# HGRN2's second head requests its state and rows behind columns that GpSimd writes; units 0 and 1 update their samples later

## Chip, cores and metric

The kernel runs on one core of a Trainium2 chip. The metric is the device time of one execution in microseconds. A run of the kernel before and one of the changed kernel are compared by the median over rounds on the same chip.

## What is computed

One inference step of a decoder layer for two groups that share the weights: a prompt of 16 meta and 256 prompt tokens, and 8 samples of one new token each, which bring recurrent states from earlier. Together they are 280 columns (in the code LP = 272 of the prompt, NS = 8 of the samples). The layer is a half feed-forward, the mixer, and a second half feed-forward, each with a layer norm. The mixer is what matters here:

```python
q_r, k_r, v_r, g_r, q_h, f_h, i_h, g_h, a_r, a_h = jnp.split(x @ w_in, N_PROJ, axis=-1)
f = lb + (1.0 - lb) * jax.nn.sigmoid(f_h.astype(jnp.float32))
k_h = to_heads((1.0 - f).astype(x.dtype), H_HG)
s_ret, o_r = retention_chunk(s_ret, q_r, k_r, v_r)
s_hg, o_h = hgrn2_chunk(s_hg, q_h, k_h, i_h, logf)
y = jax.nn.sigmoid(a_r) * o_r + jax.nn.sigmoid(a_h) * o_h
return y @ w_out, s_ret, s_hg
```

For each sample and each of the 16 HGRN2 heads the state of 128x128 becomes S' = f S + k v (an outer product of the new key and value), is written out, and gives the sample's output q S'. The 8 retention heads do the same with states of 256x256 and a fixed decay. The prompt goes through the chunked form of both and also leaves its last states.

## The kernel before

**Stages.** The span divides into the first feed-forward (up to about 745 us), the mixer's input projections with all of its recurrent work (745 to 1794), the output projection (to 1882), and the second feed-forward. Weights come from HBM in pieces of 128x1024 float32 (`raw`, 512 KB, three buffers). ACT rounds each to the matmul's format (`whi`, line 188), DVE makes the remainder (`wlo`, line 189), and PE runs 24 matmuls on it (line 218), three for each of 128 rows by 128 columns: whi with the high and the low part of x, wlo with the high part. All ten projections are made this way; their accumulators are called `pj_q_r`, `pj_i_h` and so on (r: retention, h: HGRN2).

**Units and threads.** The projections are made in eight units, u = 0 to 7. A unit covers 256 columns of each projection, one retention head and two HGRN2 heads (h = 0, 1). The recurrent work of a unit runs in two generators: `mix_hg(u, ...)`, started when a unit's `i_h` is ready, and `mix_ret(u, ...)`, started when its `v_r` is. A hook of the projections' loop, `pump`, goes on with the running generators after each step of six matmuls; `yield n` in a generator means that its next part comes n steps later. So the yields fix where the generators' matmuls stand between those of the projections.

**Order on the engines.** PE's order is the program's. On DVE, ACT and GpSimd (POOL) a scheduler orders instructions by what they depend on and by priority, and SP, which requests nearly all DMAs, has one queue in order: a request that has to wait holds all those behind it, the weights among them.

**The HGRN2 generator** (`mix_hg`). K and Q are scaled level by level with products of forget gates. A burst of small matmuls (`pl`, lines 823 and 849) makes the scores, which DVE copies into `acch` under masks (`fill`, lines 828 and 834) and ACT copies for the larger blocks (`keep`). `load(h)` requests the states of the 8 samples of head h (`smh`, 512 KB, line 769); `values(h)` requests the samples' value rows, repeated over the 128 partitions (`vbh`, 512 KB, line 772). The tiles of `smh` and `vbh` have two buffers each, which they share with the scaled queries `Qm` and with copies of K (`kept`). `turned(h)` transposes the scaled keys of head h (`ptk`, copied by ACT to `kth`, line 968). `gate()` transposes the samples' gates and keys (`ptm`) and prepares the first block's keys (`km`, line 255). `samples(h)` updates the 8 sample states of a head, each with a scaling on ACT (line 983) and a multiply-add on DVE (line 984), and requests the write of the new states (`out_sgs`, line 987). Then come the prompt's states (`pst`, `Sh`, lines 1013 to 1018), the product of the queries with the samples' new states (`pq`), and the prompt's output (`po`).

**Two paths.** Units 2 to 7 are called steady: they turn the keys of both heads first, then call the gate, then update head 0, and four steps later head 1. Units 0 and 1 call the gate first, and then turn and update head by head, two steps apart.

**The retention generator** (`mix_ret`), on the same engines: updates of its sample states (`smr`, lines 1180 to 1186, with repeated rows `vbr`), the samples' scores (`pqr`, then `scr`, line 240, and `sc`, lines 255, 723 and 724), their outputs (`osr`, centred at lines 1069 to 1071), and the output accumulator `por`: per head four matmuls of the prompt (line 1214), one of the samples' own values with `sc`, and one that adds `osr` (line 741).

Of the kernel before, what the change touches and what calls it, by code (L numbers as in the profile page):

```python
# [128 lines left out]
def trunk(ctx: ExitStack, tc: tile.TileContext, A, O):  # L129
    nc = tc.nc  # L130
# [12 lines left out]
    def mx_bank(name):  # L143
        return ps_m.tile([P, 512], F32, tag="mx", name=name)
# [135 lines left out]
    class Norm:  # L280
# [96 lines left out]
        def first(self, block, outs, x0s):  # L377


            n = self.n  # L380

            def hook(k):
                if k == 5:
                    self.stats()

            dense(block, KC, outs, xh, xl, [slice(x0, n + 2) for x0 in x0s], hook)
            ys = self.corrected(outs, x0s)
            for c in range(KC):
                d = self.d[c]
                sub(d, d, self.mean)  # L390
                nc.vector.scalar_tensor_tensor(
                    out=d, in0=d, scalar=self.g[:, c : c + 1], in1=self.r, op0=ALU.mult, op1=ALU.mult)
            return ys

        def second(self, block, outs, x0s, into=()):
            dense(block, KC, outs, xh, xl, [slice(x0, self.n + 2) for x0 in x0s])
            self.normalise()
            return self.corrected(outs, x0s, into)
# [148 lines left out]
    with tc.tile_pool(name="yp", bufs=1) as yp:  # L547
# [7 lines left out]
        with tc.tile_pool(name="mp", bufs=1) as mp:  # L555
# [7 lines left out]
            def tmp(name, shape=(P, T), bufs=1, dt=F32, tag=None):  # L563
                if name in rows:
                    rows[name] = rows[name][1:] + rows[name][:1]
                    return rp.tile(list(shape), dt, tag=rows[name][-1], name=name)
                return mp.tile(list(shape), dt, tag=tag or name, name=name, bufs=bufs)
# [80 lines left out]
            def evacuate(n, c0, c1, o0, o1, b0, b1):  # L648
# [14 lines left out]
                elif n == "i_h":  # L663
                    v = st.pop("i_h", None)
                    if v is None:
                        v = tmp("v", (P, 2, T))
                        nc.scalar.copy(v[:, 0, :], o0)
                        nc.scalar.copy(v[:, 1, :], o1)

                    start(mix_hg(c0 // 2, st["f"], st["k"], st["q"], v), {0: 20, 2: 46}.get(c0, 4))  # L670
                elif n in ("q_r", "k_r"):
                    sc, w, x0 = (1.0, TL, NMETA) if n == "q_r" else (KSC, T, 0)
# [48 lines left out]
            def upper_upper_lower(out, x, at=0):  # L721
                n = x.shape[0]
                nc.scalar.copy(out[:n], x)
                nc.scalar.copy(out[32 : 32 + n], x)
                sub(out[64 : 64 + n], x, out[at : at + n].bitcast(F32))
# [20 lines left out]
            def mix_hg(u, f, k, q, v):  # L746

                calm = 2
# [13 lines left out]
                acc = tmp("acch", (P, 2 * SEQ))  # L762
                sms, vbs = [], []

                def load(h):

                    sms.append(tmp("smh", (P, NS, P), bufs=2))
                    vbs.append(tmp("vbh", (P, NS, P), bufs=2))
                    nc.sync.dma_start(sms[h], A["sg"][2 * u + h])

                def values(h):
                    nc.sync.dma_start(vbs[h], vrow[h].partition_broadcast(P))


# [21 lines left out]
                def join(s):  # L796
                    _, m, t2 = sides(s)
                    Ts[2 * s] = tmp(f"T{2 * s}", (P, 2, m))
                    mul(Ts[2 * s], t2[:, :, :, 0], t2[:, :, :, 1])
# [25 lines left out]
                def fill(half, s, h):  # L825
                    a = acc[:, 2 * P * h : 2 * P * (h + 1)]
                    if s == 1:
                        nc.vector.tensor_tensor(
                            out=a.rearrange("p (b j c) -> p b j c", b=2, j=4),
                            in0=half[:, :, 48:].unsqueeze(2).to_broadcast([P, 2, 4, 32]),  # L830
                            in1=ident.rearrange("p (j c) -> p j c", j=4).unsqueeze(1).to_broadcast([P, 2, 4, 32]), op=ALU.mult)
                    for i, (sl, mi) in enumerate(((s, MASKS[s][0]), (2 * s, MASKS[2 * s][0]), (2 * s, MASKS[2 * s][1]))):
                        n = 16 // sl
                        nc.vector.copy_predicated(
                            a.rearrange("p (b j n t s) -> p b j n t s", b=2, j=4, t=2, s=sl)[:, :, :, :, 1, :],
                            msk[:, mi, :P].rearrange("p (b j n s) -> p b j n s", b=2, j=4, s=sl),
                            half[:, :, 16 * i : 16 * i + 16].rearrange("p b (n s) -> p b n s", s=sl).unsqueeze(2).to_broadcast([P, 2, 4, n, sl]))
# [15 lines left out]
                def keep(pl, s):  # L853
                    if s == 64:
                        for b in range(2):
                            nc.scalar.copy(
                                acc[:s, :].rearrange("p (h b n s) -> p h b n s", h=2, b=2, s=s)[:, :, b, 1, :],
                                pl[b * s : (b + 1) * s, : 2 * s].rearrange("p (h s) -> p h s", h=2))
                    else:
                        for j in range(0, 128 // s, 2):  # L860
                            nc.scalar.copy(
                                acc[j * s : (j + 1) * s, :].rearrange("p (x n s) -> p x n s", x=4, s=s)[:, :, j + 1, :],
                                pl[j * s : (j + 1) * s, : 4 * s].rearrange("p (x s) -> p x s", x=4))
# [20 lines left out]
                steady = u > 1  # L884
# [57 lines left out]
                scale_k(64)  # L942
                scale_q(64)
                join(64)
                for todo in (load, values):
                    for h in range(2):
                        todo(h)
                for h in range(2):
                    if u:
                        fill(first(h), 1, h)  # L950
                    fill(second(h), 4, h)
                    yield 4
                for s in (16, 32, 64):
                    keep(tops[s], s)
                yield 2 if steady else 8 if u else 4
                Tt = Ts[2 * LEVELS[-1]]
                on = tmp("on_h", (P, 2, TL), bufs=2)
                on_h[u] = on
                kts = []

                def turned(h):
                    kt = tmp("kth", (P, 2, P), bufs=2)
                    kts.append(kt)
                    pt = mx_bank("ptk")
                    for b in range(2):
                        t0 = NMETA + b * P
                        nc.tensor.transpose(pt[:, b * P : (b + 1) * P], K[:, h, t0 : t0 + P], ident)
                    nc.scalar.copy(kt, pt[:, : 2 * P].rearrange("p (b f) -> p b f", b=2))

                def gate():  # L970
                    pt = mx_bank("ptm")
                    x = pt[:64, :P]
                    nc.tensor.transpose(x, meta.rearrange("p h t -> p (h t)"), ident)
                    for i in range(2):
                        nc.gpsimd.tensor_copy(meta[:, :, NMETA + NS * i : NMETA + NS * (i + 1)], fk[:, i])
                    for i in range(2):
                        upper_upper_lower(km[:, i, :], x[32 * i : 32 * i + NMETA], 32 * i)

                def samples(h):
                    vb, sm = vbs[h], sms[h]  # L980
                    for b in range(NS):
                        at = NMETA + b
                        nc.scalar.activation(sm[:, b, :], sm[:, b, :], AF.Copy, scale=meta[:, h, at : at + 1])
                        nc.vector.scalar_tensor_tensor(
                            out=sm[:, b, :], in0=vb[:, b, :], scalar=meta[:, h, at + NS : at + NS + 1], in1=sm[:, b, :],
                            op0=ALU.mult, op1=ALU.add)
                    nc.sync.dma_start(O["sgs"][2 * u + h], sm)

                if steady:
                    turned(0)  # L990
                    yield 2
                    turned(1)
                    yield 4
                    gate()
                    samples(0)
                    yield 4
                    samples(1)
                    yield 6
                else:
                    gate()  # L1000
                    yield 7 if u else 6
                    for h in range(2):
                        turned(h)
                        samples(h)
                        yield 2
                    yield 12 + calm if u else 8

                Ss = []
                for h in range(2):
# [9 lines left out]
                            out=S[:, b + 1, :], in0=S[:, b, :], scalar=Tt[:, h, b : b + 1],  # L1019
                            in1=pst[:, (b + 1) * P : (b + 2) * P], op0=ALU.mult, op1=ALU.add)  # L1020
                    nc.sync.dma_start(O["sgp"][2 * u + h], S[:, 2, :])
                yield 53 if steady else 10
                pq = mx_bank("pq")
                for h in range(2):
                    for b in range(NS):
# [30 lines left out]
                calm = calm if u else 0  # L1056
# [308 lines left out]
```

## Time and profile before

| | us |
|---|---|
| runs | 2593.94, 2594.21, 2598.13 |
| median | 2594.21 |
| the profiled execution | 2599.28 |
| its span | 2597.5 |
| PE busy in it | 2564.2 |
| DVE busy | 1703.4 |
| ACT busy | 1392.9 |
| POOL busy | 42.0 |

The span is the time between the first and the last instruction of the profiled execution; the execution's own time has a start and an end around it. The profiled execution is one of its own, some 5 us longer than the median of the runs. PE's busy time is modelled: a matmul of 280 columns is listed with 0.28 us but the next one starts 0.12 us later. A row of a timeline gives the start, the duration, the engine, the line, the operation with its output and inputs, the shapes, the count, and in brackets how long the engine was idle before and whose end released it. In a table of windows stand busy times by engine, the granted clock of PE, the DMA engines' share and their rate.

### The profile page before, as it was taken

The numbers are of one execution on the slowest core, as the hardware profiler recorded it, in microseconds if no ns is written. First come the engines' busy times: TensorE is split into PE (matmuls) and PEld (weight loads), VectorE is DVE, ScalarE is ACT, GpSimd is POOL, SyncE is SP. The second block draws the span as 40 slices with busy tenths as digits, with TensorE's granted clock in tenths as the row PEclk, the third lists the DMA queues.
The fourth block names the chain that finished last, engine by engine and source line by source line (L and its number), as shares of the span: only waits on it lengthen the run. The fifth ranks groups of instructions, "written<-read, shape, count | busy, mean of one in ns | idle before, by whom it ended". The sixth has DMA issues, their size and how long they took to land.

```text
span 2597.5 us, 56210 instructions
## 1 busy us (share of the span) xinstructions
PE 2564.2 (99%) x23424; PEld 2544.3 (98%) x23424; DVE 1703.4 (66%) x2827; ACT 1392.9 (54%) x2186; POOL 42.0 (2%) x120
## 2 busy tenths in 40 slices
PE   9999999999999999999999999999999999999999
PEld 9999999999999889999999999999999999999998
DVE  6544454565579788777777777777985555556555
ACT  5444444444456667666666666665564444444444
POOL 0000000000000000000000000000000000000000
PEclk9999999999999999999999999999999999999999
DMA  7555555555566776767686868576556666666664
GB/s 241 186 184 183 186 185 183 184 184 183 185 198 209 237 263 217 263 200 265 196 269 196 269 196 268 195 250 188 194 187 199 196 195 196 195 195 194 196 195 148
DMA packets 156896, 536.26 MB, mean 206 GB/s; under 512 B 17952, under 2 KB 25952, under 8 KB 156640
## 3 DMA queue, kind: packets, MB, share of 16 engines
q1 hardware_dynamic: 156352, 532.37, 63.5%
q8 instruction: 183, 3.00, 0.5%
q14 instruction: 73, 0.60, 0.1%
q10 hardware_dynamic: 288, 0.29, 0.0%
HBM read 501.99 MB, written 30.61 MB: 205 GB/s over the span
## 4 chain that ended last, share of the span: by engine, by line
PE 90%; DVE 5%; ACT 2%; issue 1%; DMA 1%; SPq 0%; POOL 0%; DVEq 0%; ACTq 0%
PE up L218 34%; PE dn L218 18%; PE pj_k_r L218 3%; PE pj_g_r L218 3%; PE pj_q_r L218 3%; PE wo L218 3%; PE pj_a_r L218 3%; PE pj_v_r L218 3%; PE pj_g_h L218 3%; PE pj_a_h L218 3%; PE pj_q_h L218 3%; PE pj_i_h L218 3%; PE pj_f L218 3%; DVE wlo L189 2%; DMA raw<-in_w_up 1%
## 5 line engine op out<-in xcount | busy, mean ns | idle before, releaser
L189 DVE TENSOR_TENSOR wlo<-raw,whi 128x1024 fp32r<-128x1024 f32 (+1 forms) x869 | 1061.9, 1222 | 763.5 <-ACT whi L188 758.9
L188 ACT CAST whi<-raw 128x1024 fp32r<-128x1024 f32 (+1 forms) x870 | 905.4, 1042 | 922.2 <-PE up L218 411.6
L218 PE MATMUL up<-xh,wlo 128*128 128x280 f32 (+1 forms) x2624 | 725.9, 280 | 0.6 <-DVE wlo L189 0.6
L218 PE MATMUL up<-xh,whi 128*128 128x280 f32 (+1 forms) x2624 | 726.1, 280 | 0.0
L218 PE MATMUL up<-xl,whi 128*128 128x280 f32 (+1 forms) x2624 | 725.5, 280 | 0.0
L218 PEld LDWEIGHTS up<-xh,wlo 128*128 128x128 f32 x2624 | 492.6, 189 | 1.2 <-DVE wlo L189 1.2
L218 PEld LDWEIGHTS up<-xh,whi 128*128 128x128 f32 x2624 | 493.0, 189 | 0.0
L218 PEld LDWEIGHTS up<-xl,whi 128*128 128x128 f32 x2624 | 492.8, 189 | 0.0
L218 PE MATMUL dn<-hh,whi 128*128 128x280 f32 (+1 forms) x1376 | 384.7, 280 | 0.0
L218 PE MATMUL dn<-hh,wlo 128*128 128x280 f32 (+1 forms) x1376 | 384.3, 279 | 0.0
L218 PE MATMUL dn<-hl,whi 128*128 128x280 f32 (+1 forms) x1376 | 384.3, 279 | 0.0
L218 PEld LDWEIGHTS dn<-hh,whi 128*128 128x128 f32 x1376 | 260.1, 189 | 0.1
L218 PEld LDWEIGHTS dn<-hl,whi 128*128 128x128 f32 x1376 | 260.1, 189 | 0.1
L218 PEld LDWEIGHTS dn<-hh,wlo 128*128 128x128 f32 x1376 | 260.1, 189 | 0.0
L218 PE MATMUL pj_k_r<-xh,whi 128*128 128x280 f32 x256 | 75.5, 295 | 0.0
L218 PE MATMUL pj_g_r<-xh,whi 128*128 128x264 f32 x256 | 74.0, 289 | 0.0
L218 PE MATMUL pj_k_r<-xh,wlo 128*128 128x280 f32 x256 | 73.5, 287 | 0.0
L218 PE MATMUL pj_k_r<-xl,whi 128*128 128x280 f32 x256 | 73.5, 287 | 0.0
L218 PE MATMUL pj_v_r<-xh,whi 128*128 128x280 f32 x256 | 73.3, 286 | 0.0
L218 PE MATMUL pj_g_h<-xh,whi 128*128 128x264 f32 x256 | 72.8, 284 | 0.0
L218 PE MATMUL pj_v_r<-xh,wlo 128*128 128x280 f32 x256 | 72.4, 283 | 0.3 <-DVE wlo L189 0.3
L218 PE MATMUL pj_q_r<-xl,whi 128*128 128x264 f32 x224 | 64.1, 286 | 8.7 <-issue 8.7
(417 smaller groups left out, 5277.4 us busy)
## 6 DMA issues: line engine op xcount, KB each, us to landing
raw<-in_w_up SPq DMA_DIRECT2D x343, 512.0 KB, 4.2
raw<-in_w_in SPq DMA_DIRECT2D x320, 512.0 KB, 4.1
raw<-in_w_dn SPq DMA_DIRECT2D x172, 512.0 KB, 3.4
smr<-in_sr SPq DMA_DIRECT2D x32, 512.0 KB, 5.0
out_srs<-smr SPq DMA_DIRECT2D x32, 512.0 KB, 6.9
raw<-in_w_out SPq DMA_DIRECT2D x32, 512.0 KB, 3.5
vbr<-vrd SPq DMA_DIRECT2D x32, 256.0 KB, 4.3
smh<-in_sg SPq DMA_DIRECT2D x16, 512.0 KB, 6.1
```

Source lines behind the costliest of these rows:

```text
L188: nc.scalar.copy(hi[:, j:jn, :], raw[:, j:jn, :])
L189: nc.vector.tensor_tensor(out=lo[:, j0:j1, :], in0=raw[:, j0:j1, :], in1=hi[:, j0:j1, :].bitcast(F32), op=ALU.subtract)
L218: nc.tensor.matmul(o, w, t, start=start, stop=stop)
```

## The change

The second head's state is requested behind a copy on GpSimd of one column of `acch` into the state's tile; so its request can't start before the fills that write that column have ended. The request itself moves in the program from behind the score burst to behind the first head's fills. The second head's rows are requested behind a copy of one column of `kth` into their tile, and in the program behind `turned(1)`. Since the DMA writes the whole tile afterwards, the copied values are not used. This adds two copies of 128x1 in each unit. Units 0 and 1 take the steady order with pauses of their own: turn both heads, rows of head 1, 11 or 10 steps later the gate and head 0, six steps later head 1. The later pauses (before the prompt's states and before `pq`) are set anew, and in units 2 to 7 the gate comes one step later (5 for 4) with one step less before `pq` (52 for 53).

```diff
--- before.py
+++ after.py
@@ -766,9 +766,13 @@
 
                     sms.append(tmp("smh", (P, NS, P), bufs=2))
                     vbs.append(tmp("vbh", (P, NS, P), bufs=2))
+                    if h:
+                        nc.gpsimd.tensor_copy(sms[h][:, 0, :1], acc[:, 31:32])
                     nc.sync.dma_start(sms[h], A["sg"][2 * u + h])
 
                 def values(h):
+                    if h:
+                        nc.gpsimd.tensor_copy(vbs[h][:, 0, :1], kts[h][:, 0, :1])
                     nc.sync.dma_start(vbs[h], vrow[h].partition_broadcast(P))
 
 
@@ -942,17 +946,18 @@
                 scale_k(64)
                 scale_q(64)
                 join(64)
-                for todo in (load, values):
-                    for h in range(2):
-                        todo(h)
+                load(0)
+                values(0)
                 for h in range(2):
                     if u:
                         fill(first(h), 1, h)
                     fill(second(h), 4, h)
                     yield 4
+                    if h == 0:
+                        load(1)
                 for s in (16, 32, 64):
                     keep(tops[s], s)
-                yield 2 if steady else 8 if u else 4
+                yield 15 if u == 1 else 2
                 Tt = Ts[2 * LEVELS[-1]]
                 on = tmp("on_h", (P, 2, TL), bufs=2)
                 on_h[u] = on
@@ -986,24 +991,16 @@
                             op0=ALU.mult, op1=ALU.add)
                     nc.sync.dma_start(O["sgs"][2 * u + h], sm)
 
-                if steady:
-                    turned(0)
-                    yield 2
-                    turned(1)
-                    yield 4
-                    gate()
-                    samples(0)
-                    yield 4
-                    samples(1)
-                    yield 6
-                else:
-                    gate()
-                    yield 7 if u else 6
-                    for h in range(2):
-                        turned(h)
-                        samples(h)
-                        yield 2
-                    yield 12 + calm if u else 8
+                turned(0)
+                yield 2
+                turned(1)
+                values(1)
+                yield (11, 10, 5)[min(u, 2)]
+                gate()
+                samples(0)
+                yield (6, 6, 4)[min(u, 2)]
+                samples(1)
+                yield (4, 5, 6)[min(u, 2)]
 
                 Ss = []
                 for h in range(2):
@@ -1019,7 +1016,7 @@
                             out=S[:, b + 1, :], in0=S[:, b, :], scalar=Tt[:, h, b : b + 1],
                             in1=pst[:, (b + 1) * P : (b + 2) * P], op0=ALU.mult, op1=ALU.add)
                     nc.sync.dma_start(O["sgp"][2 * u + h], S[:, 2, :])
-                yield 53 if steady else 10
+                yield (8, 6, 52)[min(u, 2)]
                 pq = mx_bank("pq")
                 for h in range(2):
                     for b in range(NS):
```

Line numbers of the changed kernel differ from those of the kernel before by a few: the update of line 984 stands at 989, that of 1186 at 1183, `osr` of 1071 at 1068.

**DVE in unit 0, from a weight split to the centring of `osr`, before:**

```order
L189 TENSOR_TENSOR wlo_10437<-raw_10435,whi_10436 128x8x128
L984 SCALAR_TENSOR_TENSOR smh<-vbh,meta,smh 128x128 x5
L240 TENSOR_TENSOR scr_8637<-pqr,dtab 16x16
L984 SCALAR_TENSOR_TENSOR smh<-vbh,meta,smh 128x128 x2
L255 TENSOR_TENSOR sc_8642<-scr_8637,sc_8642 16x16
L984 SCALAR_TENSOR_TENSOR smh<-vbh,meta,smh 128x128 x4
L189 TENSOR_TENSOR wlo_10491<-raw_10489,whi_10490 128x8x128
L1069 TENSOR_REDUCE cen<-osr 128x1
L240 TENSOR_TENSOR K<-K,f 128x272
L1070 TENSOR_SCALAR cen<-cen 128x1
L240 TENSOR_TENSOR K<-K,T_10883 128x136x2
L1071 TENSOR_TENSOR osr<-osr,cen 128x256
```

And now, from the split ahead of the scores to the first updates:

```order
L189 TENSOR_TENSOR wlo_10422<-raw_10420,whi_10421 128x8x128
L240 TENSOR_TENSOR scr_8637<-pqr,dtab 16x16
L255 TENSOR_TENSOR sc_8642<-scr_8637,sc_8642 16x16
L1066 TENSOR_REDUCE cen<-osr 128x1
L1067 TENSOR_SCALAR cen<-cen 128x1
L1068 TENSOR_TENSOR osr<-osr,cen 128x256
L189 TENSOR_TENSOR wlo_10476<-raw_10474,whi_10475 128x8x128
L759 COPY fk<-f 128x16
L760 COPY fk<-k 128x16
L189 TENSOR_TENSOR wlo_10534<-raw_10532,whi_10533 128x8x128
L255 TENSOR_TENSOR km<-ptm,km 16x128
L989 SCALAR_TENSOR_TENSOR smh<-vbh,meta,smh 128x128 x3
```

The sample updates (984, now 989) stood ahead of and between `scr`, `sc` and `osr`; now the three come first, and the updates follow two and three weight splits later. Two scalings of K for unit 1 (line 240), which stood between `cen` and `osr`, now stand ahead of the rows shown.

**DVE in unit 1, from the updates of head 0 and 1 to `osr`, before:**

```order
L984 SCALAR_TENSOR_TENSOR smh<-vbh,meta,smh 128x128 x7
L189 TENSOR_TENSOR wlo_11897<-raw_11895,whi_11896 128x8x128
L984 SCALAR_TENSOR_TENSOR smh<-vbh,meta,smh 128x128 x6
L240 TENSOR_TENSOR scr_8637<-pqr,dtab 16x16
L240 TENSOR_TENSOR gt<-gs,pj_g_h_11601 128x264
L255 TENSOR_TENSOR sc_8642<-scr_8637,sc_8642 16x16
L240 TENSOR_TENSOR gt<-gt,gs 128x264
L1069 TENSOR_REDUCE cen<-osr 128x1
L704 SCALAR_TENSOR_TENSOR gt<-gt,ngt,on_h 128x264
L1070 TENSOR_SCALAR cen<-cen 128x1
L252 TENSOR_TENSOR y<-y,gt 128x264
L1071 TENSOR_TENSOR osr<-osr,cen 128x256
```

And now, from the centring of `osr` on (`scr` and `sc` stand just ahead):

```order
L1066 TENSOR_REDUCE cen<-osr 128x1
L252 TENSOR_TENSOR y<-y,gt 128x264
L1067 TENSOR_SCALAR cen<-cen 128x1
L1068 TENSOR_TENSOR osr<-osr,cen 128x256
L226 TENSOR_TENSOR yl_8613<-y,yh_8610 128x264
L189 TENSOR_TENSOR wlo_11923<-raw_11921,whi_11922 128x8x128
L742 COPY on_r<-por 128x8 x2
L189 TENSOR_TENSOR wlo_11979<-raw_11977,whi_11978 128x8x128
L255 TENSOR_TENSOR km<-ptm,km 16x128
L989 SCALAR_TENSOR_TENSOR smh<-vbh,meta,smh 128x128 x3
L252 TENSOR_TENSOR sqr<-sqr,sq_11895 128x264
L255 TENSOR_TENSOR km<-ptm,km 16x128
```

Here, too, the 16 updates moved behind `osr`, by two weight splits and the copies of `por`. Those of retention (1186), which came after the fills of `acch`, now stand among the fills.

**SP in unit 5, where the second head's state and rows are requested, before:**

```order
L772 DMA vbh<-vh0d 128x1024
L185 DMA raw_18247<-in_w_in 128x1024
L769 DMA smh<-in_sg 128x1024
L185 DMA raw_18305<-in_w_in 128x1024
L769 DMA smh<-in_sg 128x1024
L772 DMA vbh<-vh1d 128x1024
L185 DMA raw_18335<-in_w_in 128x1024
L185 DMA raw_18383<-in_w_in 128x1024
L185 DMA raw_18413<-in_w_in 128x1024
```

And now:

```order
L776 DMA vbh<-vh0d 128x1024
L185 DMA raw_18232<-in_w_in 128x1024
L771 DMA smh<-in_sg 128x1024
L185 DMA raw_18300<-in_w_in 128x1024
L771 DMA smh<-in_sg 128x1024
L185 DMA raw_18347<-in_w_in 128x1024
L185 DMA raw_18395<-in_w_in 128x1024
L776 DMA vbh<-vh1d 128x1024
L185 DMA raw_18425<-in_w_in 128x1024
```

The state of head 1 keeps its place between weight requests (but waits for its GpSimd copy there); the rows of head 1 (`vbh<-vh1d`) moved from right behind it to behind two more weight requests.

## Prediction

> **What bounds the kernel now.** I read the page's busy times, then the waits by engine, then the timeline around each wait of TensorE (PE).
>
> ```profile
> span 2597.5 us, 56210 instructions
> PE 2564.2 (99%) x23424; PEld 2544.3 (98%) x23424; DVE 1703.4 (66%) x2827; ACT 1392.9 (54%) x2186; POOL 42.0 (2%) x120
> PE pj_q_r L218 <- issue: 14.6, 6, 3.5
> PE por L741 <- DVE osr L1071: 3.6, 1, 3.6
> ```
>
> PE is the bound, so only what PE loses can be won. Its larger waits in the mixer are of two kinds: the waits of the retention output `por`, one of which is shown and all of which lie in units 0 and 1; and "issue" waits in `pj_q_r`, 14.6 us, which no engine released. Here is unit 0, PE first and DVE behind it.
>
> ```profile
> 867.41 0.84 PE L1214 MATMUL por<-dtab,vtr 128*128 128x256 f32 x4
> 869.01 0.25 PE L1214 MATMUL por<-sc,vs 128*128 128x16 f32 x1 [0.77 <-ACT sc L724]
> 872.86 0.45 PE L741 MATMUL por<-ident,osr 128*128 128x128 f32 x1 [3.60 <-DVE osr L1071]
> ...
> 865.99 1.39 DVE L984 SCALAR_TENSOR_TENSOR smh<-vbh,meta,smh 128x128 f32<-128x128 f32 x5
> 867.41 0.16 DVE L240 TENSOR_TENSOR scr<-pqr,dtab 16x16 f32<-16x16 f32 x1
> 867.50 0.59 DVE L984 SCALAR_TENSOR_TENSOR smh<-vbh,meta,smh 128x128 f32<-128x128 f32 x2
> ...
> 868.90 1.14 DVE L984 SCALAR_TENSOR_TENSOR smh<-vbh,meta,smh 128x128 f32<-128x128 f32 x4
> 870.00 1.22 DVE L189 TENSOR_TENSOR wlo<-raw,whi 128x1024 fp32r<-128x1024 f32 x1
> 872.30 0.41 DVE L1071 TENSOR_TENSOR osr<-osr,cen 128x256 f32<-128x256 f32 x1
> ```
>
> PE is ready for `por` at 867.41. The chain it needs (scr, sc on DVE and ACT, then cen and osr) is threaded between sample updates (L984) and one weight split (`wlo`). The updates ahead of and inside the chain take 1.39+0.59+1.14 = 3.1 us. The clock then falls:
>
> ```profile
> 872.90:877.90 5.00, 5.00 (x23) 4.82 (x24) 3.13 (x8) 2.97 (x8) 0.21 (x1) 0.54 0.89 312
> ```
>
> The eighth field is the granted clock: 0.54 over the 5.0 us in which PE works again, so (1-0.54)x5.0 = 2.3 us more lost. Unit 1 shows the same picture without a slow stretch:
>
> ```profile
> 967.14 0.84 PE L1214 MATMUL por<-dtab,vtr 128*128 128x256 f32 x4
> 969.63 0.25 PE L1214 MATMUL por<-sc,vs 128*128 128x16 f32 x1 [1.65 <-DVE sc L255]
> 971.63 0.30 PE L741 MATMUL por<-ident,osr 128*128 128x128 f32 x1 [1.75 <-ACT yh L225]
> ...
> 960.55 0.88 DVE L1186 SCALAR_TENSOR_TENSOR smr<-vbr,sro,smr 128x256 f32<-128x256 f32 x2
> ...
> 964.12 1.93 DVE L984 SCALAR_TENSOR_TENSOR smh<-vbh,meta,smh 128x128 f32<-128x128 f32 x7
> 967.10 1.66 DVE L984 SCALAR_TENSOR_TENSOR smh<-vbh,meta,smh 128x128 f32<-128x128 f32 x6
> 968.79 0.16 DVE L240 TENSOR_TENSOR scr<-pqr,dtab 16x16 f32<-16x16 f32 x1
> 971.06 0.42 DVE L1071 TENSOR_TENSOR osr<-osr,cen 128x256 f32<-128x256 f32 x1
> ```
>
> With unit 0 the four waits come to 0.77+3.60+1.65+1.75 = 7.8 us. The second wait here is put down to ACT's yh, but osr ends at 971.48, 0.15 us before the matmul starts: osr was last. In unit 6, whose updates already stand elsewhere, the same head has no wait:
>
> ```profile
> 1607.66 0.84 PE L1214 MATMUL por<-dtab,vtr 128*128 128x256 f32 x4
> 1608.24 0.27 PE L1214 MATMUL por<-sc,vs 128*128 128x16 f32 x1
> ```
>
> **The change, part by part.**
>
> *Unit 0, samples later.* DVE's order now has scr, sc, cen, osr ahead of all 16 updates. Taking the 3.1 us of updates off the osr at 872.71 leaves about 869.6; two K scalings of the next unit and a split now stand ahead of the chain, but so did 1.39 us of updates and a split before, so scr starts at about 864 to 866. From scr to osr, without updates and split, the chain takes 872.71-867.41-0.59-1.14-1.22 = 2.4 us. So osr comes at about 866.4 to 868.4, against a need some 0.7 us behind 867.41 (0.58 us from the first matmul to the sc one in unit 6 above). Removed: 0.77+3.60 = 4.4 us of waiting, and with it the slow 2.3 us: 6.7 us. Bounds: 3.0 if a wait of a microsecond and more stays and the clock still falls; 6.7 at most. I take 6.5. What is late next: the updates themselves, 16 x 0.29 = 4.6 us of DVE (1.14 for four), now among splits and the q_r rotation, followed by the product `pq` eight pumps behind `pst`. In the stretch from 872.90, quoted above, DVE works 3.13 of 5.00 us, and it is 66% busy over the span, so some 13 us take them in; `pq` comes later than that. If a split is late by one update block, 1.1 us, it comes off this term.
>
> *Unit 1, samples later.* The same 1.65+1.75 = 3.4 us are at stake, but here DVE is near full:
>
> ```profile
> 940.00:955.00 15.00, 14.32 (x124) 13.93 (x124) 11.70 (x29) 9.56 (x17) 0.57 (x4) 1.00 0.85 298
> 955.00:970.00 15.00, 13.13 (x124) 11.51 (x122) 14.38 (x37) 10.97 (x32) 0.00 (x0) 1.00 0.97 310
> 970.00:985.00 15.00, 13.37 (x114) 13.35 (x115) 10.87 (x28) 10.42 (x20) 0.00 (x0) 1.00 0.90 312
> ```
>
> (PE, weight loads, DVE, ACT, POOL, then clock, DMA share, GB/s.) The updates of heads 0 and 1, 4.5 us by the rows above, go from the second stretch into the third, 10.87+4.5 = 15.4 of 15.0; and the retention rows now requested earlier pull the second half of the retention updates (eight, 0.88 for two) forward, into the first: 11.70+3.5 = 15.2. Both overflow by a fraction that must push into neighbours, where each split late beyond its lead costs PE. Then the Q scalings of unit 2 must be done before its scores burst; here is the last one and that burst's first matmul:
>
> ```profile
> 1013.28 0.42 DVE L240 TENSOR_TENSOR Q<-Q,T 128x256 f32<-128x256 f32 x1
> ...
> 1014.94 0.29 PE L823 MATMUL pl<-Qm,k 128*32 128x48 f32 x8
> ```
>
> The slack is 1.2 us. From -3.4 (all won) to +1.5 (a split late by one 1.22 us in each of the overfull stretches, less nothing won); I take -2.0.
>
> *Requests behind POOL columns, all units.* Sixteen copies of 128x1 on POOL. The nearest row is the 128x16 copy:
>
> ```profile
> L975 POOL COPY meta<-fk 128x16 f32<-128x16 f32 x16 | 3.6, 253 | 171.5 <-PE ptm L973 171.5
> ```
>
> 16 x 0.25 = 4 us on an engine that is 2% busy, hidden; if nothing hid them, 4 us of delayed requests, not of PE. What they move is two requests on SP, with the weight requests queued behind. In unit 4:
>
> ```profile
> 1406.25 0.43 SPq L769 DMA_DIRECT2D smh<-in_sg  x1
> 1406.72 0.43 SPq L772 DMA_DIRECT2D vbh<-vh1d  x1
> 1414.96 13.96 SPq L185 DMA_DIRECT2D raw<-in_w_in  x5
> ...
> 1407.48 2.46 DVE L834 COPY_PREDICATED acch<-msk,pl 128x128 f32<-128x128 uint8 x10
> ...
> 1419.99 0.37 ACT L968 COPY kth<-ptk 128x256 f32<-128x256 f32 x1
> ...
> 1428.49 1.92 DVE L984 SCALAR_TENSOR_TENSOR smh<-vbh,meta,smh 128x128 f32<-128x128 f32 x7
> ...
> smh<-in_sg SPq DMA_DIRECT2D x2, 512.0 KB, 6.7
> ```
>
> The state waits for fills, ten of which end by 1409.9, and the next weight request isn't due before 1414.96: free. The rows wait for the kth copy, 1420.4, plus a POOL copy; SP's order has two weight requests ahead of them, and the five of the row stand 3.5 us apart, so the third is due at about 1422: SP isn't held. Requested at 1420.7 and, like the states, landed 6.7 us later (median, last row) they are there at 1427.4, against a need at 1428.49 or later. I take 0, bounds -8 and +16 (rivals two and three).
>
> **Sum**, against the profiled execution (2599.28 us, span 2597.5): -6.5-2.0+0 = -8.5, 2590.8. That execution is 5.1 us above the median shown, 2594.21, so the forecast is **2586 us**; by the terms' bounds without the requests, 2582 to 2592.
>
> **Rivals.**
>
> *One, the wait moves to the weight splits.* For it: the sums of 15.4 and 15.2 in 15.0 above, and 0.97 DMA share where weights must land. Against: unit 0 has room. Unit 1 then ends at +1.5 and unit 0 wins 4.5: 2594.2-3.0 = 2591.
>
> *Two, the "issue" stalls shrink in units 3 to 7.* The largest rows of all waits, and after them the clock falls too:
>
> ```profile
> 1410.19 0.38 PE L218 MATMUL pj_q_r<-xl,whi 128*128 128x264 f32 x1 [3.14 <-issue]
> ...
> q8 instruction: 1, 0.02, 2.7%
> ...
> DMA packets 202, 0.75 MB, mean 339 GB/s; under 512 B 23, under 2 KB 23, under 8 KB 201
> ```
>
> The last two rows are of the window from 1408.0 to 1410.2: one packet of instruction code moved, and all queues together 339 GB/s; from 1403 to 1408 no code did. State and rows of head 1 (1 MB, 1406.25 and 1406.72) enter the queue just before that packet. If they hold it up, 1 MB at the 339 GB/s of that window is 3 us; a third of it saved in five units, 5 us, and in one or two of them the slow stretch as well, 2.3 in unit 0, make 8: 2578. Against: they enter less than a microsecond before PE stops (1410.19-3.14 = 1407.05), while what was in the queue ahead of them, the rows of head 0 among it, stays where it was. By the Trainium skill, "DMA: Bandwidth & Descriptors", section on queues, rings and completion order, each DMA engine alternates between queue rows packet by packet, so a code packet would never stand behind a megabyte of the other queue, and the requests moved would bring nothing. The 3.14 us wait ahead of that one packet says that it does wait for something; what, the trace doesn't tell.
>
> *Three, slower: the second head's rows come late.* DVE is in order, so an update of head 1 that waits for them holds the split queued behind it. It decides if they land well over 7.8 us after the request (1428.49-1420.7) instead of 6.7: then, once the splits have used up their lead, PE waits about one group of weights. A group is due every (1428.92-1414.96)/4 = 3.5 us by the raw row; by three quarters of one, 2.7 us, in each of units 2 to 7: +16, 2586+16 = 2602. For: DMA is 0.90 and 0.97 busy in the stretches of unit 1 above. Against: that is now a time with 1 MB less asked for at once.
>
> *Four, the order is changed but not the end:* osr waits for something other than the updates, such as ACT's sc (0.77 above), and the waits return with another releaser: 2594.
>
> **Chances.** Forecast 0.50, one 0.17, two 0.12, three 0.13, four 0.08. A measurement of this kernel can tell about 0.2%, 5.2 us, from no change: below 2589.0 is faster, above 2599.4 slower. The forecast's own range is 2582 to 2590, mostly faster (0.46); with two and a little of one, 0.61. Four, most of one and the rest: same, 0.27. Three, less its mild end: 0.12. The range that leaves out 2 in 10 runs from 2577 to 2598.
>
> **What would show it.** Right: no `por` row in the waits of units 0 and 1; the clock at 1.00 from 865 to 880; L984 of unit 0 behind osr on DVE; "issue" of `pj_q_r` still near 14.6; raw requests of units 2 to 7 at unchanged pitch. Wrong: new `wlo` waits in `pj_q_h`, `pj_i_h` or `pj_f` around 950 to 1015 (one), an "issue" sum under 10 (two), L984 waiting for DMA `vbh` with PE waiting for `wlo` (three), or `por` waits released by ACT (four).

## The result and the profile after

| | us |
|---|---|
| before, median of 14 runs | 2597.74 (2593.32 to 2604.61) |
| changed, median of 14 runs | 2587.8 (2584.26 to 2595.21) |
| ratio | 0.9966, 95% interval 0.9956 to 0.9976 |
| profiled execution of the changed kernel | 2588.29, span 2586.5 |

The interval is 6 to 11 us of gain. The forecast was 8 to 9, with 2586 as the time. (The kernel before had 2594.21 as the median of its first three runs; over 14 runs it is 2597.74.)

First the waits of PE in the changed kernel (engine, line, what it waited for; then us in total, times, the longest):

```profile
PE pj_q_r L218 <- issue: 15.1, 6, 3.1
PE pw L515 <- DVE eps_h L163: 1.0, 1, 1.0
PE pvr L237 <- DVE rlo L226: 0.8, 1, 0.8
PE pj_f L218 <- DVE wlo L189: 0.7, 1, 0.7
```

No row of `por` is left. The "issue" waits are there as before, 15.1 us for 14.6. A new wait stands on `pvr`, the retention's normalisation in unit 1, 0.8 us (0.2 to 0.6 us, or none, in the other executions with unit 1 changed).

Next the places in unit 0 and, behind the "...", unit 1 where `por` waited, in the timeline of PE and of DVE:

```profile
866.82 0.84 PE L1211 MATMUL por<-dtab,vtr 128*128 128x256 f32 x4
867.40 0.27 PE L1211 MATMUL por<-sc,vs 128*128 128x16 f32 x1
867.53 0.32 PE L741 MATMUL por<-ident,osr 128*128 128x128 f32 x1
...
958.68 0.32 PE L741 MATMUL por<-ident,osr 128*128 128x128 f32 x1
```

```profile
862.18 0.15 DVE L240 TENSOR_TENSOR scr<-pqr,dtab 16x16 f32<-16x16 f32 x1
862.60 0.17 DVE L255 TENSOR_TENSOR sc<-scr,sc 16x16 fp32r<-16x16 f32 x1 [0.27 <-ACT sc L723]
863.23 0.42 DVE L1066 TENSOR_REDUCE cen<-osr 128x1 f32<-128x256 f32 x1 [0.46 <-ACT osr L1202]
863.87 0.42 DVE L1068 TENSOR_TENSOR osr<-osr,cen 128x256 f32<-128x256 f32 x1
...
868.14 0.88 DVE L989 SCALAR_TENSOR_TENSOR smh<-vbh,meta,smh 128x128 f32<-128x128 f32 x3
...
958.08 0.43 DVE L1068 TENSOR_TENSOR osr<-osr,cen 128x256 f32<-128x256 f32 x1
```

In unit 0, `osr` ends at 864.29 and is needed at 867.53: 3.2 us to spare, and the first update comes at 868.14. In unit 1 it ends at 958.51 and is needed at 958.68: 0.17 us to spare. The windows around these places (PE, weight loads, DVE, ACT, POOL; granted clock; DMA share; GB/s):

```profile
865.00:880.00 15.00, 15.00 (x129) 14.90 (x128) 13.74 (x38) 13.73 (x34) 0.33 (x2) 1.00 0.85 316
940.00:955.00 15.00, 14.92 (x149) 13.70 (x148) 11.34 (x23) 8.73 (x20) 0.89 (x2) 1.00 0.95 322
955.00:970.00 15.00, 14.19 (x118) 13.89 (x117) 11.88 (x30) 11.44 (x30) 0.33 (x2) 1.00 0.85 294
970.00:985.00 15.00, 15.00 (x155) 14.68 (x154) 12.90 (x36) 11.93 (x26) 0.21 (x1) 1.00 0.69 234
```

The clock is 1.00 throughout. DVE, third of the five times, is busy 11 to 14 of 15 us in each stretch. The work of unit 1 runs earlier than before, though, and a stretch further ahead shows DVE full:

```profile
932.00:947.00 15.00, 14.92 (x157) 14.64 (x151) 14.97 (x37) 10.13 (x19) 0.62 (x3) 1.00 0.99 330
```

Where the time went shows in the first matmul of the same group in both executions. First the rows of before, then the change's own:

```profile
858.08 0.28 PE L218 MATMUL pj_q_r<-xh,whi 128*128 128x264 f32 x1
895.14 0.28 PE L218 MATMUL pj_v_r<-xh,whi 128*128 128x280 f32 x1
993.41 0.28 PE L218 MATMUL pj_i_h<-xh,whi 128*128 128x280 f32 x1
1020.10 0.28 PE L218 MATMUL pj_k_r<-xh,whi 128*128 128x280 f32 x1
1683.94 0.28 PE L218 MATMUL pj_v_r<-xh,whi 128*128 128x280 f32 x1
```

```profile
857.83 0.28 PE L218 MATMUL pj_q_r<-xh,whi 128*128 128x264 f32 x1
887.59 0.28 PE L218 MATMUL pj_v_r<-xh,whi 128*128 128x280 f32 x1
981.67 0.28 PE L218 MATMUL pj_i_h<-xh,whi 128*128 128x280 f32 x1
1009.98 0.28 PE L218 MATMUL pj_k_r<-xh,whi 128*128 128x280 f32 x1
1672.88 0.28 PE L218 MATMUL pj_v_r<-xh,whi 128*128 128x280 f32 x1
```

| stretch | before, us | changed, us | difference | forecast |
|---|---|---|---|---|
| unit 0's outputs (`pj_q_r` to `pj_v_r`) | 37.06 | 29.76 | -7.3 | -6.5 |
| unit 1's outputs (to `pj_i_h`) | 98.27 | 94.08 | -4.2 | -2.0 |
| score burst of unit 2 (to `pj_k_r`) | 26.69 | 28.31 | +1.6 | 0 |
| units 3 to 7 (to their last `pj_v_r`) | 663.84 | 662.90 | -0.9 | 0 |

The four make -10.8 of the 11.0 us between the two spans. They compare one execution of each kernel; what of them recurs in other executions is said in the part on the prediction. The +1.6 is an "issue" wait in unit 2, where before none of that size stood:

```profile
1007.96 0.38 PE L218 MATMUL pj_q_r<-xl,whi 128*128 128x264 f32 x1 [1.85 <-issue]
```

### The profile page after: what moved, and what is told of

It is laid out like the page before. It is cut to its first block, busy times and chain, and to the rows that moved or that the text cites. A ratio compares the mean times of both kernels' runs of the same rounds, so it can differ in the third digit from the quotient of the medians.

```text
span 2586.5 us, 56251 instructions
## 1 busy us (share of the span) xinstructions
PE 2560.9 (99%) x23424; PEld 2541.4 (98%) x23424; DVE 1701.5 (66%) x2827; ACT 1392.2 (54%) x2186; POOL 50.4 (2%) x136
## 4 chain that ended last, share of the span: by engine, by line
PE 93%; DVE 4%; issue 1%; DMA 1%; ACT 1%; POOL 0%; SPq 0%; ACTq 0%; DVEq 0%
PE up L218 36%; PE dn L218 18%; PE pj_q_r L218 3%; PE pj_g_r L218 3%; PE pj_a_r L218 3%; PE pj_k_r L218 3%; PE wo L218 3%; PE pj_g_h L218 3%; PE pj_a_h L218 3%; PE pj_v_r L218 3%; PE pj_i_h L218 3%; PE pj_q_h L218 3%; PE pj_f L218 3%; DVE wlo L189 1%; DVE xl L421 0%
## 5 line engine op out<-in xcount | busy, mean ns | idle before, releaser
L218 PE MATMUL pj_v_r<-xl,whi 128*128 128x280 f32 x256 | 72.3, 283 | 0.0
```

The lines of the kernel that those rows point to most:

```text
L218: nc.tensor.matmul(o, w, t, start=start, stop=stop)
```

## The experiments

All ratios are to the kernel before, run beside each group, over five rounds.

**One part at a time.** Three kernels have the change in units 2 to 7 alone, in unit 0 alone, and in unit 1 alone. In each, this stands around the changed lines, with `new` as named (shortened: the columns, the order of the requests and the earlier pauses hang on `new` too, and the old branches stay for the other units):

```diff
+new = steady        # or: u == 0, or: u == 1
-if steady:
+if new:
     turned(0)
     yield 2
     turned(1)
+    values(1)
...
-yield 53 if steady else 10
+yield (8, 6, 52)[min(u, 2)] if new else 53 if steady else 10
```

Units 2 to 7 alone:

> Units 2 to 7 as in the changed kernel (second head's state and rows requested behind the POOL columns, gate one step later), units 0 and 1 as before. Theory (all of the gain is in the por waits of units 0 and 1): time within 2 us of before, ratio 0.9993 to 1.0007, the por waits of 7.8 us unchanged, issue waits of pj_q_r 14 to 15 us in sum. Rival (part of the gain comes from the requests): 4 us and more faster, ratio under 0.9985, with issue waits under 11 us.

Measured: ratio 1.0007 (0.9998 to 1.0015), 2599.93 against 2599.03. PE's waits in its profile:

```profile
PE pj_q_r L218 <- issue: 14.3, 6, 3.6
PE por L741 <- DVE osr L1093: 3.6, 1, 3.6
PE por L741 <- ACT yh L225: 1.8, 1, 1.8
...
PE por L1236 <- DVE sc L255: 1.6, 1, 1.6
```

So the moved requests and the gate's step in these units are worth nothing by themselves, as forecast; rival two, by which they shorten the "issue" waits, falls.

Unit 0 alone:

> Unit 0 as in the changed kernel, all other units as before. Theory: the por wait (4.4 us) and the slow clock behind it (2.3 us) go, 6.5 to 7.5 us faster, ratio 0.9971 to 0.9975. Rival (the two units' waits hang together, unit 1 gets back what unit 0 wins): under 4 us faster.

Measured: ratio 0.9983 (0.9974 to 0.9991), 2 to 7 us faster. Only the two `por` waits of unit 1 are left in its profile, 1.8 and 1.6. From the first matmul of unit 0's `pj_q_r` to that of its `pj_v_r` it took 29.8 us, as the whole change did, so 7.3 us are won on the spot; the span won 4.8. The time of all runs, 5.2 us less by the medians, lies between the theory's 6.5 to 7.5 and the rival's "under 4", and the interval reaches into both. The rest of the 7.3 us was lost elsewhere in this execution. The largest piece, 1.7 us, lies behind the `por` waits of unit 1, which stay: this time the clock fell there, to 0.51, and the stretch around them, from the first matmul of `pj_f` to that of `pj_i_h`, took 33.0 us for 31.4. The window behind the second of the two waits:

```profile
964.80:968.30 3.50, 3.50 (x16) 3.32 (x16) 1.65 (x5) 1.98 (x4) 0.00 (x0) 0.51 0.91 315
```

Another 0.9 us lies just ahead of unit 0's `pj_q_r`, where `pj_i_h` waits twice for `wlo` instead of once. The "issue" waits, 15.4 us in sum with one of 4.2 (longest before: 3.5), differ from kernel to kernel by a microsecond each. What recurs is the stretch itself: from `pj_q_r` to `pj_v_r` it takes 29.8 us in each of the nine profiled executions with unit 0 changed, and 36.2 to 37.4 us in the four without.

Unit 1 alone:

> Unit 1 as in the changed kernel, all other units as before. Theory after the first trace: 3.4 us of por waits and about 0.8 us of wlo waits ahead of them go, 2 to 4.5 us faster, ratio 0.9983 to 0.9992. The prediction's smaller estimate, in which crowded DVE gives part back: 1 to 2.5 us faster, with new wlo waits in units 1 and 2.

Measured: ratio 0.9986 (0.9975 to 0.9996), 1 to 6.5 us faster. The `por` waits of unit 1 are gone, those of unit 0 remain. By the ratio it is 3.6 us, in the theory's range; the interval doesn't exclude the smaller estimate. No new `wlo` wait stands behind the changed place. Two are longer than before: `pj_i_h` (2.5 for 0.9) at 850 and 857, ahead of all that this kernel changes, and `pj_g_h` (1.0 for 0.6) at 952.34, among the retention updates that now come earlier on DVE; a small part of what the smaller estimate feared may be there.

**Without the columns.**

> The changed kernel without the sixteen POOL copies: the second head's rows are requested early again in units 2 to 7, behind its state. Theory (columns worth nothing): within 2 us of the changed kernel, ratio to before 0.996 to 0.9975, issue waits 14 to 16 us. Rival (requests in the queue hold up instruction code): slower than the changed kernel by 3 to 8 us, issue waits above 17 us.

```diff
-if h:
-    nc.gpsimd.tensor_copy(sms[h][:, 0, :1], acc[:, 31:32])
 nc.sync.dma_start(sms[h], A["sg"][2 * u + h])
...
-if h:
-    nc.gpsimd.tensor_copy(vbs[h][:, 0, :1], kts[h][:, 0, :1])
 nc.sync.dma_start(vbs[h], vrow[h].partition_broadcast(P))
```

Measured: ratio 0.9967 (0.9956 to 0.9979), the same as with them. The "issue" waits are 17.1 us in its one profile, 2 more than with the columns and above the rival's 17, but the clock fell for less time behind them; in the total no difference shows, so the rival falls by its time. The scheduler puts the rows of head 1 right behind its state again, as before. As far as the time tells, the sixteen copies can go.

**The call alone.** Is it the place of `samples()` in the program that moves the updates on DVE?

> The kernel before, with the samples() calls of units 0 and 1 five and ten steps later in the program and nothing else: the gate stays where it was. The order on DVE shows that the scheduler leaves unit 0's updates around scr, sc and osr as before, since they are ready once the gate's copies are there, and moves about half of unit 1's behind osr. Theory (the order on DVE sets the por waits, and the gate, not the call, sets that order): unit 0's por waits stay near 4.4 us, unit 1's 3.4 us shrink to 1 to 2.5 us, 0 to 3 us faster than before. Rival (the call's place in the program is what matters): 7 to 10 us faster, as the changed kernel.

```diff
 gate()
 yield 7 if u else 6
 for h in range(2):
     turned(h)
-    samples(h)
     yield 2
-yield 12 + calm if u else 8
+yield 8 if u else 3
+samples(0)
+yield 2
+samples(1)
+yield 4 if u else 3
```

Measured: ratio 0.9991 (0.9979 to 1.0003); by time it can't be told from no change. The `por` rows can be: those of unit 0 stay, in unit 1 one is left of two.

```profile
PE por L741 <- DVE osr L1074: 5.5, 2, 3.6
...
PE por L1217 <- ACT sc L724: 0.6, 1, 0.6
```

Unit 0: 3.6+0.6 as before; unit 1: 5.5-3.6 = 1.9 where 3.4 stood. So the call's place alone doesn't move unit 0's updates, and moves unit 1's in part. What goes along with them is the gate, the work that makes the updates ready: its first matmul (`ptm`) in unit 0 starts at 855.82 before, at 856.16 here and at 865.36 in the changed kernel, and the first update on DVE follows at 861.83, 861.96 and 868.14. No run moved the gate alone.

**The "issue" waits.** They are the largest wait in both kernels, and the second group asked what they wait for. Beside the changed kernel itself:

> The changed kernel, unaltered, for comparison in this group: ratio to before 0.9956 to 0.9976 as measured, issue waits of pj_q_r about 15 us.

Measured: ratio 0.9955 (0.9939 to 0.997), 2587.38 us, "issue" 14.0.

The first head's rows later:

> The changed kernel, and in units 2 to 7 the first head's rows, too, are requested behind a POOL column after the first fills, so they are no longer in the queue when the score burst asks for instruction code. Theory A (the code packet waits for the first head's rows): issue waits fall from 15 us to under 8 us and the slow clock behind them goes, 6 to 14 us faster than the changed kernel, ratio 0.991 to 0.994. Theory B (the burst of 320 small matmuls uses up code faster than it can be fetched, whatever is in the queue): issue waits stay at 13 to 17 us, ratio 0.9956 to 0.9976.

```diff
+elif steady:                  # in values(h), for h == 0
+    nc.gpsimd.tensor_copy(vbs[h][:, 0, :1], acc[:, 31:32])
...
 load(0)
-values(0)
+if not steady:
+    values(0)
...
 fill(second(h), 4, h)
+if steady and h == 0:
+    values(0)
 yield 4
```

Measured: ratio 0.9913 (0.9897 to 0.9929), 2577.08 us, 10.3 under the changed kernel beside it.

The first head's state later as well:

> As the kernel with the first head's rows behind a POOL column, and the first head's state behind one as well. Theory A: no more than 1 to 2 us better than with the rows alone, since the state enters the queue 1.2 us after the code is asked for. If the state holds the code up, issue waits fall by a further 3 us and more. Theory B: issue waits stay at 13 to 17 us. In all: a loss of some us if the first head's samples then wait for their state.

```diff
-if not steady:
-    values(0)
+if not steady:
+    load(0)
+    values(0)
...
 if steady and h == 0:
+    load(0)
     values(0)
```

(with the column for `sms[0]` too). Measured: ratio 0.9916 (0.9901 to 0.993), 2577.77 us: the state adds nothing.

The score burst in pieces:

> The changed kernel, with the score burst of units 2 to 7 in four pieces one projection step (0.7 us) apart, ending where it ended before; the requests are left alone. Theory B (code used up too fast): 2.1 us more between the first and the last small matmul, issue waits fall from 15 us to 3 to 6 us, 8 to 14 us faster than the changed kernel. Theory A (the queue): the code asked for earlier comes earlier only by as much, issue waits fall to 9 to 12 us, 3 to 6 us faster.

```diff
 if steady:
-    yield 6
+    yield 3
 for h in range(2):
     if u:
         pls[h] = mx_bank("pl")
         blocks(first(h), Q1, k[:, :, NMETA:], h, q)
+    if steady:
+        yield 1
...
 for h in range(2):
     blocks(second(h), Q4, K4, h)
+if steady:
+    yield 1
```

Measured: ratio 0.9912 (0.9898 to 0.9927), 2577.11 us. The largest wait in the lists of the changed kernel and of these three, in the order of the runs above:

```profile
PE pj_q_r L218 <- issue: 14.0, 6, 3.4
```

```profile
PE pj_q_r L218 <- issue: 8.6, 6, 2.3
```

```profile
PE pj_q_r L218 <- issue: 7.5, 6, 1.7
```

```profile
PE pj_q_r L218 <- issue: 2.8, 4, 1.2
```

With the rows out of the way 14.0 becomes 8.6; with the burst in pieces 2.8. These sums are of one execution each, and in the eight profiled executions of kernels that leave the burst and the first head's rows alone they run from 11.0 to 17.1 us; 8.6, 7.5 and 2.8 lie below all of them. For the rows theory A gave under 8 and B 13 to 17; for the pieces A gave 9 to 12 and B 3 to 6. So each theory is near in its own run (8.6 just above A's range, 2.8 just below B's) and wrong in the other's; the times, 10 us under the changed kernel in both, lie in A's range for the rows and in B's for the pieces.

What the waits end with can be read in the traces' DMA records. In unit 5 of the changed kernel one packet of 16 KB on the queue of instruction code moves from 1398.23 to 1399.19, and PE, idle since 1398.10, goes on at 1400.42. The trace has 183 such packets, one in 14 us, so the two would seldom meet by chance. But so it is everywhere: in the eleven profiled executions that have such waits, 64 in all, PE goes on 1.2 to 1.6 us after the end of a code packet. The packet itself mostly takes 0.9 to 1.3 us. In the changed kernel it starts 3.8 us after the first matmul of the burst (mean of units 3 to 7 in the execution of this group), with the rows later 2.8 us, with the state later as well 2.6 us. With the burst in pieces the packet is no earlier, but the burst takes 4.9 us instead of 1.9. So both causes are there: the dense burst is over before the next code has come, and the rows in the queue let that code come later. (When the code is asked for, on which the expectation for the state rests, no trace shows.)

The gain with the rows, 10 us, is larger than the wait saved, 5.4 us, because the slow clock behind the waits goes too: the mean granted clock of the profiled executions is 0.996 in the changed kernel and 0.998 with the rows later, and 0.002 of 2578 us is 5 us. For the windows from 1100 to 1794 us, first of the changed kernel as profiled at the beginning, then of the one with the pieces, the clock is 0.99 and 1.00:

```profile
1100.00:1794.00 694.00, 680.39 (x6751) 671.50 (x6750) 521.87 (x1015) 447.87 (x823) 28.95 (x76) 0.99 0.70 228
```

```profile
1100.00:1794.00 694.00, 690.65 (x6854) 679.10 (x6853) 528.38 (x1021) 452.16 (x828) 29.36 (x76) 1.00 0.70 231
```

PE is busy 10.3 us longer in the same stretch; that is the wait alone, 13.3 us in this window (15.1 less the 1.85 of unit 2) for 2.8.

**Both together.**

> First head's rows behind a POOL column and the score burst in four pieces, on top of the changed kernel. If the wait is one latency that either can cover: issue waits under 1.5 us, time 1 to 4 us below the 2577 us of each alone, ratio 0.989 to 0.991. If the two add: cannot exceed what is left of issue waits with the burst in pieces, 2.8 us, since no slow clock is left either.

Its edit is the sum of the two above. Measured: ratio 0.9901 (0.9882 to 0.992), 2572.98 us, with no "issue" row left at all:

```profile
PE pj_i_h L218 <- DVE wlo L189: 1.2, 2, 0.8
PE pw L515 <- DVE eps_h L163: 1.0, 1, 1.0
PE pj_f L218 <- DVE wlo L189: 0.7, 1, 0.7
```

> As the kernel with rows and burst in pieces, with the first head's state behind a POOL column as well. Within 1.5 us of it, unless the first head's samples wait for their state, which would show as DVE or ACT waiting for the DMA of smh and cost a few us.

Measured: ratio 0.9904 (0.9885 to 0.9923), 2573.00 us, the same. By the ratios (0.9912 and 0.9901) the rows add 2.9 us to what the pieces bring, and 2.8 us of waits had been left; but the two intervals overlap, and the runs are of different groups. The kernel with both beats the one before by 1.0%, some 26 us, and the changed one by about 14.

## Why the prediction was right

The end was right: 2586 forecast, 2587.8 measured, in its own range of 2582 to 2590. That the time agrees to 2 us is in part luck: the kernel before, from whose first three runs the forecast started, is 3.5 us slower over all runs, and the gain is larger than forecast by 1.7 us (9.9 by the medians for 8.2). Within the profiled execution the larger gain in units 0 and 1 was partly given back in unit 2. By its steps:

*Unit 0, -6.5.* Measured -7.3 on the spot, 0.6 beyond the bound of 6.7; against the three other executions that have unit 0 as before it is 6.5 to 7.6. The mechanism is shown: DVE's updates stood ahead of `osr`; with them behind, `por` has no wait and the clock doesn't fall (1.00 in the window from 865, with all 15.00 us of PE busy). The time for `osr` was put too late, at 866.4 to 868.4; it was ready at 864.29. The chain from `scr` to `osr` took 864.29-862.18 = 2.1 us, near the 2.4 worked out; what was wrong was the start of `scr`, 862.18 for "864 to 866": only two K scalings and one split, which starts at 861.04, stood ahead of it on DVE.

*Unit 1, -2.0.* The mechanism was right and the size was off: measured -4.2 in this execution. The step that was mis-sized is "both overflow by a fraction that must push into neighbours". The stretches of 15.2 and 15.4 us that it summed came out at 11.34 and 12.90. The sum had moved whole blocks of updates into stretches fixed in time, without taking out what leaves them, while all work there now runs some 7 to 12 us earlier. Into the stretch from 940 to 955 came 3.49 us of retention updates, but 2.07 us of others had left it; and of the 4.64 us of the samples' updates only 1.49 lie in the stretch from 970 to 985, the rest ahead of it.

The worry itself had ground, in two places that the sum didn't name. `osr` has 0.17 us to spare. And DVE is full from 932 to 947 (14.97 of 15.00 us, above): there PE had no wait in this execution, but 1.0 us for `wlo` in `pj_g_h` in the second execution of the same kernel, and 2.0 us in the kernel with the first head's rows later.

So the -4.2 has a part that recurs and one that doesn't. From the first matmul of `pj_f` to that of `pj_i_h` it is 993.41-962.03 = 31.4 us before and 981.67-952.86 = 28.8 now: the 3.4 us of `por` less the 0.8 on `pvr`. It is 28.2 to 28.6 in the second execution, without the columns and with unit 1 alone, and 33.0 in the two kernels of the first group that leave unit 1 as it was, where the clock fell behind `por`. (The prediction's "without a slow stretch" held for the one execution it read.) The other 1.6 us lie ahead, from `pj_v_r` to `pj_f` (962.03-895.14 = 66.9 before, 952.86-887.59 = 65.3 now), and can't be put down to the change: the second execution takes 67.1.

*The requests, 0.* Shown twice: nothing in units 2 to 7 alone (1.0007), and nothing from taking out the columns (0.9967). The copies of `kth`'s column took longer than estimated, and are hidden as said; POOL's groups in the changed kernel:

```profile
L775 POOL COPY vbh<-kth 128x1 f32<-128x1 f32 x8 | 7.5, 937 | 70.8 <-ACT kth L973 70.8
...
L770 POOL COPY smh<-acch 128x1 f32<-128x1 f32 x8 | 1.5, 187 | 98.8 <-issue 59.0 <-DVE acch L838 20.4 <-DMA smh<-in_sg 12.5
```

9.0 us for the sixteen where 4 had been put. In unit 5 (the rows that the prediction put into unit 4 belong to unit 5) SP's timeline in the changed kernel now reads

```profile
1401.14 0.33 SPq L771 DMA_DIRECT2D smh<-in_sg  x1
1404.22 3.94 SPq L185 DMA_DIRECT2D raw<-in_w_in  x2
1410.21 0.33 SPq L776 DMA_DIRECT2D vbh<-vh1d  x1
```

with the next weights requested 0.4 us behind: not held, as forecast.

*The "issue" waits stay near 14.6.* 15.1. Not foreseen was the one in unit 2, 1.85 us for 0.2 before. In the first group, where two matmuls that normally start 0.11 us apart are 1.1 to 1.9 us apart, it is 0.8 to 1.6 us, also in the kernel with unit 0 alone, whose unit 2 is as before; so its size varies with more than the change in unit 2, and what brings it is open.

*The rivals.* One (the wait moves to the weight splits) fell: no new `wlo` wait stands in `pj_q_h`, `pj_i_h` or `pj_f` from 950 to 1015; the 1.0 us in `pj_g_h` of the second execution is what is left of it. Two fell as it was put, by the second head's requests, though the queue does matter: it is the first head's rows, which stand ahead of the code, as the argument against the rival had said. When 512 KB leave the queue, the wait falls from 14.0 to 8.6 us and the code packet starts 1 us earlier, so the backlog does count here. By the Trainium skill, "DMA: Bandwidth & Descriptors", section on queues, rings and completion order, each DMA engine alternates between queue rows packet by packet; by that a code packet would not stand behind the other queue's megabyte, and the runs differ from it. The wait for code is 14 us in six units, and 2.8 with the burst in pieces. The Trainium skill, "Runtime: NRT & Kernel Launch", section on instruction fetch mechanics, calls the cost of a new code block mostly hidden; behind this burst it isn't. (The profile lists 160 matmuls and 160 weight loads in a burst; the "320 small matmuls" of the expectations are both together.) Three (rows late) and four (waits with another releaser) fell: the list of DVE's waits has none for `vbh`, and `por` has no row.

What stays open: that PE waits for code rests on the code packet that ends ahead of each of the 64 waits' ends and on both remedies working; no run changed the code fetch itself, and why a backlog on the other queue lets the code packet start later, the traces don't tell.

## What to carry to other kernels

Short chains that PE waits for (a 16x16 score, a centring) should not stand behind bulk work on an in-order engine; where a scheduler sets that order, delay what makes the bulk work ready, not only its call. When an engine's wait has no releaser and follows a dense burst of small instructions, look for code packets in the DMA records, then try spreading the burst over the work around it, and moving bulk transfers from just ahead of it to behind it. A sum over a crowded stretch must also take out what leaves it. A local gain of a few microseconds is read on the spot, since waits elsewhere scatter by as much, and in more than one execution, since a wait of half a microsecond or a fall of the clock can be there in one and not in the next.

## What was not expected

That instruction code bounds anything: 14 to 15 us of waits without a releaser, in the changed kernel six of 1.9 to 3.1 us, each behind a burst of 160 small matmuls with their weight loads, and a slow clock behind three or four of them; gone with the burst in pieces and 512 KB out of its way, 14 us in all. And a copy of one column on POOL is listed with 0.94 us where it read `kth` and 0.19 us where it read `acch`, for the same 128x1.
